# First modulation: the scale summed by columns on TensorE, the shift alone on VectorE

## The chip, the core and the metric

The kernel runs on one core of one Trainium2 chip. The metric is the device time of one execution in microseconds (us); the kernel before has a median of 1437.47 us over 3 runs (1434.62 to 1438.4). One further execution was recorded by the profiler; the rows below come from it.

Engines are written as in the profile: PE is TensorE's matmul, PEld its weight load, DVE is VectorE, ACT is ScalarE, POOL is GpSimd, SP is SyncE, which here only issues transfers.

## The reference, cut to what matters

Two layers, 512 rows of 1024 features, all float32. Each layer begins with a normalization that is modulated by a vector computed from the condition `c`:

```
ada_in = silu(c)
mod  = (ada_in @ w_ada[i] + b_ada[i]).reshape(b, 6, d)
sh_m, sc_m = mod[:, 0], mod[:, 1]
hm = rmsnorm(x, norm_mix[i]) * (1 + sc_m) + sh_m
y  = dilated_mixer(hm, a_w_in[j], ...)
```

The shift `sh_m` and the scale `sc_m` of the first layer are each a product of a vector of 1024 with a matrix of 1024 x 1024 (4 MB). Nothing of the layer can be projected before they are there, so this pair is computed first, in the function `begin`, on its own; the other ten vectors of the two layers are summed in the background later.

## The kernel before, in words

`begin` loads `x` (4 row blocks of 128), then the 8 MB of the scale's and the shift's weights. It works in two halves of 512 features. For each half there are 8 transfers of 512 KB, each with two slices of 128 of the 1024 inputs: first 4 for the scale (n = 0), then 4 for the shift (n = 1). They land in 11 buffers (6 of the tag `mix`, 5 of the tag `ada0`), so that the last five transfers of the second half wait until earlier buffers have been read.

VectorE multiplies each slice by its input (`csil`, one number per partition) and adds it into an accumulator `accs[n]` of 128 partitions (L359). The sum over the 128 partitions is left to TensorE: for each group of 128 features one product with the accumulator's 128 columns as weights and a column of ones as the moving operand (L368), so the result stands as a column, one feature per partition, in PSUM. VectorE then makes the column of scales, (1 + scale) * norm (L371), and copies the column of shifts (L373).

Between, `rows()` squares and scales `x` (ACT, L336, L340), transposes it on PE (L344, 32 products) and copies the result to `xT` (ACT, L345). When the columns of a half are there, ACT makes the high part of `h` for its four groups of 128 features (L376), and VectorE its low part (L377, L378).

After the first half's `h`, PE can begin the first projection with half of its inputs: `project_early` runs 48 products of 128 x 128 by 512 columns (L293, L294, L296: high x high, high x low, low x high) for 4 row blocks into 4 PSUM banks. The rest of that projection needs the second half's `h`. The projection's weights come in a stream (`st`): SP issues the transfers (L114), ACT makes the high part (L150) and VectorE the low part (L151); a buffer is free for the next transfer when L151 has run.

The program is written in this order, and a scheduler places each engine's instructions: earlier lines have priority, but what isn't ready by the scheduler's own reckoning is overtaken. `issue_after(last.ins)` puts L371 and L373 behind the half's last L359 on VectorE. Each engine then runs its list strictly in order.

Of the kernel before, what the change touches and what calls it, by code (L numbers as in the profile page):

```python
# [8 lines left out]
F32 = mybir.dt.float32  # L9
# [4 lines left out]
OP = mybir.AluOpType  # L14
# [3 lines left out]
P = 128  # L18
D = 1024
S = 512  # L20
KT = D // P
# [154 lines left out]
class Trunk:  # L176
# [71 lines left out]
    def cols(self, w, kt0, nk, parts, kind=""):  # L248

        n = sum(m for _, m in parts)  # L250
        src, at = [], 0
        wv = w.rearrange("(kt p) c -> p kt c", p=P)
        for c0, m in parts:
            src.append((wv[:, kt0:kt0 + nk, c0:c0 + m],
                        lambda raw, at=at, m=m: raw[:, :nk * n].rearrange("p (k c) -> p k c", c=n)[:, :, at:at + m]))
            at += m
        return (src, nk * n, kind)
# [41 lines left out]
    def begin(self, sb, first):  # L299

        nc, i, V = self.nc, self.i, self.nc.vector
        c16 = self.k.tile([16, P], F32, name="c16", tag="c16", bufs=1)
        nc.sync.dma_start(out=c16[0:8], in_=i["c"].rearrange("o (k p) -> (o k) p", p=P))
        nc.scalar.dma_start(out=c16[8:16], in_=i["norm_mix"][0].rearrange("(k p) -> k p", p=P))
        self.ident = self.k.tile([P, P], F32, name="ident")
        nc.sync.dma_start(out=self.ident, in_=i["cst"][:, C_I:C_I + P])
        xs = []
        for b in range(NB):
            x = self.k.tile([P, D], F32, name="big", tag="big", bufs=5)
            nc.sync.dma_start(out=x, in_=i["x"][0, b * P:(b + 1) * P, :])  # L310
            xs.append(x)
        self.ones = self.k.tile([P, P], F32, name="ones")
        V.memset(self.ones, 1.0)
        self.one = self.k.tile([P, 1], F32R, name="one")
        nc.scalar.activation(self.one, self.ones[:, 0:1], AF.Copy)
        accs = []
        for n in range(2):
            acc = sb.tile([P, D], F32, name="acc0", tag="acc0", bufs=2)
            nc.gpsimd.memset(acc, 0.0)
            nc.gpsimd.dma_start(out=acc[0:1, :], in_=i["b_ada"][0:1, (1 - n) * D:(2 - n) * D])  # L320
            accs.append(acc)
        t = self.bank("s")
        nc.tensor.transpose(t[:, 0:16], c16, self.ident[0:16, 0:16])
        self.csil = self.k.tile([P, 8], F32, name="csil")
        col = self.k.tile([P, 2, KT], F32, name="col")
        silu = nc.scalar.activation(self.csil, t[:, 0:8], AF.Silu)
        with self.tc.issue_after(silu.ins):
            self.exp_ln()
        V.tensor_copy(col[:, 0], t[:, 8:16])
        xT = sb.tile([P, KT, S], F32, name="xT")  # L330

        def rows():
            ss = self.small(NB, "ss4")
            for b in range(NB):
                sq = sb.tile([P, D], F32, name="sq0", tag="sq0", bufs=1)
                nc.scalar.activation(sq, xs[b], AF.Square, accum_out=ss[:, b:b + 1])  # L336
            V.tensor_scalar(ss, ss, 1.0 / D, EPS, op0=OP.mult, op1=OP.add)
            r = self.rsqrt(ss, NB)
            for b in range(NB):
                nc.scalar.activation(xs[b], xs[b], AF.Copy, scale=r[:, b:b + 1])  # L340
            for k in range(KT):
                t = self.bank("t")
                for b in range(NB):
                    nc.tensor.transpose(t[:, b * P:(b + 1) * P], xs[b][:, k * P:(k + 1) * P], self.ident)  # L344
                nc.scalar.activation(xT[:, k, :], t, AF.Copy)  # L345

        wv = i["w_ada"][0].rearrange("(k p) c -> p k c", p=P)
        for half in range(2):
            cs = slice(half * 512, half * 512 + 512)
            for n in range(2):  # L350
                for kk in range(0, KT, 2):
                    if (8 * half + 4 * n + kk // 2) % 11 < 6:
                        raw = self.k.tile([P, D], F32, name="mix", tag="mix", bufs=6)
                    else:
                        raw = sb.tile([P, D], F32, name="ada", tag="ada0", bufs=5)
                    raw = raw.rearrange("p (k c) -> p k c", c=512)
                    nc.sync.dma_start(out=raw, in_=wv[:, kk:kk + 2, (1 - n) * D + half * 512:(1 - n) * D + half * 512 + 512])
                    for k in range(2):
                        last = V.scalar_tensor_tensor(accs[n][:, cs], raw[:, k], self.csil[:, kk + k:kk + k + 1], accs[n][:, cs], op0=OP.mult, op1=OP.add)  # L359
                if half == 0 and n == 0:  # L360
                    rows()
            if half:
                self.early = self.project_early(first)
            c = slice(4 * half, 4 * half + 4)
            for n in range(2):
                t = self.bank("s")
                for k in range(4 * half, 4 * half + 4):
                    nc.tensor.matmul(t[:, k:k + 1], lhsT=accs[n][:, k * P:(k + 1) * P], rhs=self.ones[:, 0:1], start=True, stop=True)  # L368
                with self.tc.issue_after(last.ins):
                    if n == 0:  # L370
                        V.scalar_tensor_tensor(col[:, 0, c], t[:, c], 1.0, col[:, 0, c], op0=OP.add, op1=OP.mult)  # L371
                    else:
                        V.tensor_copy(col[:, 1, c], t[:, c])  # L373
            for k in range(4 * half, 4 * half + 4):
                hi, lo = self.h(k, slice(None))
                nc.scalar.activation(hi, xT[:, k, :], AF.Identity, scale=col[:, 0, k:k + 1], bias=col[:, 1, k:k + 1])  # L376
                V.tensor_scalar(xT[:, k, :], xT[:, k, :], col[:, 0, k:k + 1], col[:, 1, k:k + 1], op0=OP.mult, op1=OP.add)  # L377
                V.tensor_tensor(lo, xT[:, k, :], hi.bitcast(F32), op=OP.subtract)  # L378
            if half == 0:
                self.st.fill(2)  # L380
# [98 lines left out]
        nc.vector.tensor_scalar(g[:, 0:1], g[:, 0:1], -0.125, None, op0=OP.mult)  # L479
        return g  # L480

    def project_early(self, cols):

        w = [self.st.get(512) for _ in range(2)]
        banks = [self.bank("pj" if b < 3 else "o") for b in range(NB)]
        for b, ps in enumerate(banks):
            for j in range(2):
                self.part(ps, [(*self.h(2 * j + n, cols(b)), *w[j][n]) for n in range(2)], j == 0, False)
                if b == NB - 1:
                    self.st.done()  # L490
        return banks
# [911 lines left out]
```

## Time and profile before

| | |
|---|---|
| median of 3 runs | 1437.47 us (1434.62 to 1438.4) |
| the profiled execution's own time | 1427.06 us |
| its span, first to last instruction | 1425.3 us |
| mean granted TensorE clock | 0.966 |
| PE busy | 1311.6 us (92%) |
| DVE busy | 967.4 us (68%) |
| ACT busy | 652.4 us (46%) |
| POOL busy | 121.0 us (8%) |

The granted clock is a share of full speed: 1.00 stands for 2.4 GHz, 0.50 for 1.2 GHz. A row of a timeline gives the start, the time from there to the end of the last of its instructions, engine, line, output and inputs, shapes and the number of instructions merged; in square brackets stands the idle time before and what ended it. Products are pipelined: the next one starts before the last one's end, so the pitch from start to start is what a stream of them costs.

### The profile page before, as it was taken

What the parts mean: (1) busy time and instruction counts of PE and PEld (TensorE: products, weight loads), DVE (VectorE), ACT (ScalarE), POOL (GpSimd) and SP (SyncE); (2) the same over time, 40 slices, a digit from 0 to 9 for tenths busy, and PEclk for the clock granted to TensorE, in tenths of its full rate; (3) what the DMA queues carried; (4) which work ended last, traced back from release to release, by engine and by line L of the source; (5) the groups of instructions that cost most, each with busy time, mean ns of one, the idle gap of its engine ahead of it and who ended that gap; (6) DMA issues with size and microseconds to landing.
All of it is one profiled execution on the core that took longest, in us unless ns stands there. A gap on an engine that the chain in (4) does not pass through costs nothing. (4 is left out here: it accounts for less than half of the span.)

```text
span 1425.3 us, 20009 instructions
## 1 busy us (share of the span) xinstructions
PE 1311.6 (92%) x7017; PEld 1068.2 (75%) x7017; DVE 967.4 (68%) x1913; ACT 652.4 (46%) x1356; POOL 121.0 (8%) x120
## 2 busy tenths in 40 slices
PE   5899999999998999989979998499999999699995
PEld 4787989888996899878756665268988978566662
DVE  6875776676677676655677775486767854877772
ACT  6433544344435444443355554354554542365560
POOL 0000000000000000000032221000000000223221
PEclk9899999999999999989979999799999999899998
DMA  9465445643554445264789997413321465799981
GB/s 360 138 207 179 153 156 162 202 141 120 169 191 151 161 148 164 82 218 149 254 268 313 294 295 233 148 50 95 112 65 62 134 202 191 258 288 303 302 278 22
DMA packets 187156, 264.14 MB, mean 185 GB/s; under 512 B 23065, under 2 KB 148697, under 8 KB 187047
## 3 DMA queue, kind: packets, MB, share of 16 engines
q1 hardware_dynamic: 160742, 227.86, 48.9%
q0 software_dynamic: 8576, 16.85, 5.0%
q10 hardware_dynamic: 17728, 18.05, 4.3%
q8 instruction: 59, 0.97, 0.3%
q14 instruction: 51, 0.41, 0.1%
HBM read 249.85 MB, written 25.43 MB: 193 GB/s over the span
## 5 line engine op out<-in xcount | busy, mean ns | idle before, releaser
L293 PE MATMUL ps_pj<-hi,h 128*128 128x512 f32 (+1 forms) x1016 | 390.6, 393 | 9.6 <-ACT h L453 5.0
L294 PE MATMUL ps_pj<-lo,h 128*128 128x512 f32 (+1 forms) x1016 | 371.9, 374 | 0.0
L296 PE MATMUL ps_pj<-hi,h 128*128 128x512 f32 (+1 forms) x1016 | 290.0, 374 | 0.0
L293 PEld LDWEIGHTS ps_pj<-hi,h 128*128 128x128 f32 x1016 | 238.6, 235 | 32.7 <-ACT h L453 7.1
L294 PEld LDWEIGHTS ps_pj<-lo,h 128*128 128x128 f32 x1016 | 240.3, 237 | 14.4 <-issue 0.8
L296 PEld LDWEIGHTS ps_pj<-hi,h 128*128 128x128 f32 x1016 | 211.5, 235 | 20.0 <-issue 1.1
L150 ACT ACTIVATE hi<-raw 128x1024 fp32r<-128x1024 f32 x126 | 132.4, 1052 | 130.3 <-PE ps_pj L296 70.7
L151 DVE TENSOR_TENSOR lo<-raw,hi 128x1024 fp32r<-128x1024 f32 x126 | 151.8, 1213 | 48.1 <-ACT hi L150 46.1
L392 DVE SCALAR_TENSOR_TENSOR acc<-ada,csil,acc 128x1024 f32<-128x1024 f32 x80 | 102.6, 1283 | 69.0 <-DMA ada<-in_w_ada 68.8
L293 PE MATMUL ps_pj<-hi,xh 128*112 128x512 f32 x256 | 104.9, 410 | 2.2 <-ACT xh L453 2.2
L294 PE MATMUL ps_pj<-lo,xh 128*112 128x512 f32 x256 | 104.2, 407 | 0.0
L296 PE MATMUL ps_pj<-hi,xl 128*112 128x512 f32 x256 | 80.8, 397 | 0.0
L453 ACT ACTIVATE xh<-ps_t 128x448 fp32r<-128x448 f32 x64 | 31.8, 542 | 81.8 <-PE ps_t L448 75.7
L1235 DVE SCALAR_TENSOR_TENSOR y<-ps_s,r_ws,g_f 112x512 f32<-112x512 f32 x64 | 47.8, 748 | 28.5 <-PE ps_s L1234 28.5
L462 DVE TENSOR_REDUCE qss<-sq 128x8 f32<-128x512 f32 x64 | 43.7, 682 | 31.5 <-ACT sq L460 30.8
L460 ACT ACTIVATE sq<-ps_pj 128x512 f32<-128x512 f32 x63 | 37.1, 589 | 57.7 <-PE ps_pj L296 50.9
L151 DVE TENSOR_TENSOR lo<-h,hi 128x1024 fp32r<-128x1024 f32 x42 | 51.1, 1223 | 15.4 <-ACT hi L150 14.6
L720 PEld LDWEIGHTS ps_o<-vr,pt 128*128 128x128 f32 x480 | 58.6, 193 | 1.4
L720 PE MATMUL ps_o<-vr,pt 128*128 128x64 f32 x480 | 57.8, 272 | 0.0
L293 PEld LDWEIGHTS ps_pj<-hi,xh 128*112 128x112 f32 x256 | 45.5, 178 | 15.4 <-ACT xh L453 3.1
L296 PEld LDWEIGHTS ps_pj<-hi,xl 128*112 128x112 f32 x256 | 44.9, 176 | 15.6 <-DVE xl L454 0.6
L927 ACT ACTIVATE nl<-nl,mn 128x128 f32<-128x128 f32 (+1 forms) x64 | 35.7, 559 | 40.6 <-DVE mn L925 40.1
(280 smaller groups left out, 2176.8 us busy)
## 6 DMA issues: line engine op xcount, KB each, us to landing
ada<-in_w_ada SPq DMA_DIRECT2D x85, 512.0 KB
raw<-in_a_w_in SPq DMA_DIRECT2D x128, 256.0 KB
h<-in_w_gate SPq DMA_DIRECT2D x42, 256.0 KB
h<-in_w_up SPq DMA_DIRECT2D x42, 256.0 KB
mix<-in_w_gate SPq DMA_DIRECT2D x37, 256.0 KB
mix<-in_w_up SPq DMA_DIRECT2D x37, 256.0 KB
raw<-in_w_down SPq DMA_DIRECT2D x18, 512.0 KB
h<-in_w_down SPq DMA_DIRECT2D x18, 512.0 KB
```

The lines of the kernel that those rows point to most:

```text
L150: t.act = nc.scalar.activation(h, r, AF.Copy)
L151: nc.vector.tensor_tensor(l, r, h.bitcast(F32), op=OP.subtract)
L293: nc.tensor.matmul(out, lhsT=hi, rhs=wh, start=first and n == 0, stop=False)
L294: nc.tensor.matmul(out, lhsT=hi, rhs=wl, start=False, stop=False)
L296: nc.tensor.matmul(out, lhsT=lo, rhs=wh, start=False, stop=last and n == len(terms) - 1)
L392: nc.vector.scalar_tensor_tensor(acc, raw, self.csil[:, kt:kt + 1], acc, op0=OP.mult, op1=OP.add)
L453: self.nc.scalar.activation(hv, tv, AF.Copy)
L460: nc.scalar.activation(sq, ps, AF.Square)
L462: nc.vector.tensor_reduce(ss, sq.rearrange("p (h d) -> p h d", d=HD), axis=AX.X, op=OP.add)
L720: nc.tensor.matmul(held["o"][:, at:at + HD], lhsT=pt[:, a * P:(a + 1) * P], rhs=v, start=(m == 0), stop=(m == len(terms) - 1))
L927: nc.scalar.activation(pr[:, sl], pr[:, sl], AF.Exp, scale=-1.0, bias=mn, accum_out=held["d"][:, h * 4 + b:h * 4 + b + 1])
L1235: nc.vector.scalar_tensor_tensor(y[:, cs], yp, m["ws"][0:CAP, e:e + 1], m["g_f"][0:CAP, cs], op0=OP.mult, op1=OP.mult)
```

## The change

The scale's accumulator goes. The scale is summed on TensorE directly: each 128 x 128 block of its weights is the stationary operand and the matching column of `csil` the moving one, 8 slices x 4 groups of features = 32 products of one column for each half, accumulated in PSUM over the slices. The bias is a further small product of 4 rows (`b4`, loaded through ACT's queue). VectorE sums the shift alone, 8 L359 instead of 16 for each half. For the first half the new function `scale` is called ahead of `rows()`; for the second half `project_early` calls it ahead of its third row block.

```diff
-        accs = []
-        for n in range(2):
-            acc = sb.tile([P, D], F32, name="acc0", tag="acc0", bufs=2)
-            nc.gpsimd.memset(acc, 0.0)
-            nc.gpsimd.dma_start(out=acc[0:1, :], in_=i["b_ada"][0:1, (1 - n) * D:(2 - n) * D])
-            accs.append(acc)
+
+        acc = sb.tile([P, D], F32, name="acc0", tag="acc0")
+        nc.gpsimd.memset(acc, 0.0)
+        nc.gpsimd.dma_start(out=acc[0:1, :], in_=i["b_ada"][0:1, 0:D])
+        b4 = sb.tile([4, 2, P], F32, name="b4")
+        nc.scalar.dma_start(out=b4, in_=i["b_ada"][0:1, D:2 * D].rearrange("o (h k p) -> (o k) h p", h=2, p=P))
...
-                    for k in range(2):
-                        last = V.scalar_tensor_tensor(accs[n][:, cs], raw[:, k], self.csil[:, kk + k:kk + k + 1], accs[n][:, cs], op0=OP.mult, op1=OP.add)
-                if half == 0 and n == 0:
-                    rows()
-            if half:
-                self.early = self.project_early(first)
-            c = slice(4 * half, 4 * half + 4)
-            for n in range(2):
+                    raws += [raw[:, k] for k in range(2)]
+
+            def scale():
+
                 t = self.bank("s")
-                for k in range(4 * half, 4 * half + 4):
-                    nc.tensor.matmul(t[:, k:k + 1], lhsT=accs[n][:, k * P:(k + 1) * P], rhs=self.ones[:, 0:1], start=True, stop=True)
-                with self.tc.issue_after(last.ins):
-                    if n == 0:
-                        V.scalar_tensor_tensor(col[:, 0, c], t[:, c], 1.0, col[:, 0, c], op0=OP.add, op1=OP.mult)
-                    else:
-                        V.tensor_copy(col[:, 1, c], t[:, c])
+                nc.tensor.matmul(t[:, c], lhsT=b4[:, half], rhs=self.ident[0:4, 0:4], start=True, stop=False)
+                for kt in range(KT):
+                    for k in range(4):
+                        nc.tensor.matmul(t[:, 4 * half + k:4 * half + k + 1], lhsT=raws[kt][:, k * P:(k + 1) * P], rhs=self.csil[:, kt:kt + 1],
+                                         start=False, stop=(kt == KT - 1 and k == 3))
+                V.scalar_tensor_tensor(col[:, 0, c], t[:, c], 1.0, col[:, 0, c], op0=OP.add, op1=OP.mult)
+
+            for kt in range(KT):
+                last = V.scalar_tensor_tensor(acc[:, cs], raws[KT + kt], self.csil[:, kt:kt + 1], acc[:, cs], op0=OP.mult, op1=OP.add)
+            if half == 0:
+                scale()
+                rows()
+            else:
+                self.early = self.project_early(first, scale)
+            t = self.bank("s")
+            for k in range(4 * half, 4 * half + 4):
+                nc.tensor.matmul(t[:, k:k + 1], lhsT=acc[:, k * P:(k + 1) * P], rhs=self.ones[:, 0:1], start=True, stop=True)
+            with self.tc.issue_after(last.ins):
+                V.tensor_copy(col[:, 1, c], t[:, c])
...
-    def project_early(self, cols):
+    def project_early(self, cols, between):
...
         for b, ps in enumerate(banks):
+            if b == 2:
+                between()
```

## Rows read from the trace of the kernel before

**Rows 1.** The page's first part: busy time of each engine over the span.

```profile
PE 1311.6 (92%) x7017; PEld 1068.2 (75%) x7017; DVE 967.4 (68%) x1913; ACT 652.4 (46%) x1356; POOL 121.0 (8%) x120
```

**Rows 2.** Stretches: length, busy time of each engine (instructions), granted clock, transfers.

```profile
10.75:17.25 6.50, 2.40 (x8) 1.19 (x9) 6.29 (x13) 4.68 (x6) 0.00 (x0) 1.00 1.05 408
17.25:25.50 8.25, 8.25 (x42) 7.42 (x40) 5.90 (x9) 5.02 (x9) 0.00 (x0) 1.00 1.07 379
...
28.15:31.60 3.45, 3.45 (x10) 2.82 (x9) 3.45 (x7) 1.72 (x3) 0.00 (x0) 0.51 1.05 408
...
40.10:49.50 9.40, 2.52 (x17) 2.37 (x16) 8.84 (x13) 2.86 (x4) 0.00 (x0) 0.78 0.38 116
49.50:55.50 6.00, 5.99 (x13) 4.38 (x14) 5.97 (x10) 3.13 (x4) 0.00 (x0) 0.50 1.07 324
...
910.00:920.00 10.00, 3.00 (x11) 2.74 (x12) 6.17 (x14) 7.88 (x19) 0.00 (x0) 0.50 0.51 203
```

**Rows 3.** Timeline of PE, first half of the modulation.

```profile
17.40 1.71 PE L368 MATMUL ps_s<-ones,acc 128*128 128x1 f32 x8
18.97 5.55 PE L344 MATMUL ps_t<-ident,big 128*128 128x128 f32 x24
24.32 1.19 PE L368 MATMUL ps_s<-ones,acc 128*128 128x1 f32 x8
```

**Rows 4.** Timeline of PE, second half of the modulation.

```profile
38.77 0.40 PE L294 MATMUL ps_o<-lo,h 128*128 128x512 f32 x1
39.01 0.40 PE L293 MATMUL ps_o<-hi,h 128*128 128x512 f32 x1
...
41.52 1.05 PE L368 MATMUL ps_s<-ones,acc 128*128 128x1 f32 x8 [1.40 <-DVE acc L359]
...
49.51 0.81 PE L293 MATMUL ps_pj<-hi,h 128*128 128x512 f32 x1 [3.20 <-ACT h L376]
...
54.33 0.63 PE L293 MATMUL ps_pj<-hi,h 128*128 128x512 f32 x1
54.75 0.63 PE L294 MATMUL ps_pj<-lo,h 128*128 128x512 f32 x1
```

**Rows 5.** Timeline of PE at two other places: transposes of the same shape.

```profile
64.11 0.27 PE L655 MATMUL ps_t<-J,qn 128*128 128x128 f32 x1
64.22 0.27 PE L656 MATMUL ps_t<-ident,qn 128*128 128x128 f32 x1
...
917.00 1.97 PE L448 MATMUL ps_t<-ident,hm 128*128 128x128 f32 x8 [16.71 <-DVE hm L430]
```

**Rows 6.** Timeline of DVE: sums of the modulation, and the last column.

```profile
12.47 7.71 DVE L359 SCALAR_TENSOR_TENSOR acc<-mix,csil,acc 128x512 f32<-128x512 f32 x10
20.21 3.12 DVE L359 SCALAR_TENSOR_TENSOR acc<-ada,csil,acc 128x512 f32<-128x512 f32 x4
...
38.73 4.19 DVE L359 SCALAR_TENSOR_TENSOR acc<-mix,csil,acc 128x512 f32<-128x512 f32 x6
...
48.11 0.15 DVE L373 COPY col<-ps_s 128x4 f32<-128x4 f32 x1
```

**Rows 7.** Timeline of ACT: the first part of h, of either half.

```profile
26.00 1.51 ACT L376 ACTIVATE h<-xT,col 128x512 fp32r<-128x512 f32 x2
...
48.66 1.50 ACT L376 ACTIVATE h<-xT,col 128x512 fp32r<-128x512 f32 x2
```

**Rows 8.** Timeline of SP's queue: the second half's last five transfers.

```profile
19.79 3.50 SPq L357 DMA_DIRECT2D mix<-in_w_ada  x5
```

**Rows 9.** Line 368: engine, operation, number; shortest, median, longest ns; first and last start.

```profile
L368 PE MATMUL ps_s<-ones,acc x32: 208/250/353, 17.4 to 46.0; 128*128 128x1 f32 x32
```

**Rows 10.** Waits: who for whom, us in total, times, longest.

```profile
SPq L114 <- DVE lo L151: 11.2, 3, 9.5
...
PE ps_s L404 <- ACT ada L397: 5.2, 3, 2.3
...
PE ps_t L655 <- DVE rs_t L215: 1.6, 1, 1.6
```

More of the change, by code (lines that the diff above doesn't have):

```diff
@@ L348, in begin @@
         for half in range(2):
-            cs = slice(half * 512, half * 512 + 512)
+            cs, c = slice(half * 512, half * 512 + 512), slice(4 * half, 4 * half + 4)
+            raws = []
             for n in range(2):
```

## Prediction, made before the changed kernel was run

> **What bounds the kernel now.** I read the busy times first: PE works 92% of the span [rows 1], so time is mostly won or lost where PE waits, and work that is added to PE is time wherever PE doesn't. The change touches the first 60 us, so I cut these into stretches by the timeline of PE and asked for each engine's busy time and the granted clock in each [rows 2]. From 10.75 to 17.25 PE works 2.40 of 6.50 us: the scale's first weights are there, VectorE sums them (6.29 us of 6.50), PE idles 4.1 us. From 17.25 to 25.50 PE is full (8.25 of 8.25) with the transposes and the two groups of L368 [rows 3]; 0.5 us after the last of these ACT begins the first h, at 26.00 [rows 7]. Then PE runs the 48 products of the early projection up to 40.1. From 40.1 to 49.5 it works 2.52 of 9.40 us while VectorE is full (8.84): here VectorE is the bound, with the second half's L359 and the L151 between them [rows 2, 6]. The column of shifts comes at 48.11, h at 48.66, PE's next product at 49.51 [rows 4, 6, 7].
>
> The clock matters as much. Stretch 49.5 to 55.5 is granted 0.50, the 1.2 GHz level, after the idle 40.1 to 49.5; products of 512 columns go at a pitch of 0.42 us there (54.33, 54.75), against 0.24 at 1.00, 2.4 GHz (38.77, 39.01) [rows 2, 4]. In the first 25 us the column reads 1.00 as well, but I don't believe it there: 24 transposes take 5.55 us, 0.23 each [rows 3], eight take 1.97 us, 0.25 each, in a stretch granted 0.50 [rows 2, 5], and two at 64 us, granted 1.00, start 0.11 apart [rows 5]. So PE runs at the low level until the last transposes, although it was busy without a gap from 17.25.
>
> **What the change removes.** 16 of 32 L359. Fourteen of them took 10.83 us at 12.47 to 23.33, 0.77 each; six later ones 4.19, 0.70 each [rows 6]: 11 to 12 us off VectorE. Only the second half's 8, some 5.6 us, lie on the path. In the first half VectorE ends at 23.33 while PE goes on to 25.51 [rows 3, 6], so these 8 are worth nothing by themselves. One POOL fill and one transfer of 4 KB go too, on an engine that works 8% [rows 1]: nothing.
>
> **What it adds.** Line 368 makes 16 products in the code and 32 in the trace [rows 9]: a float32 product is two passes, each with its own load of 128 columns of weights. So the 64 new products are 128 passes, and the two of `b4` 4 more: 66 for each half, less 8 of L368 that go. A pass is the same operation as L368's (128 x 128 weights, one column), so its price is in the trace, at either level: eight at 17.40 take 1.71 us and the last of them alone 0.35, so (1.71 - 0.35) / 7 = 0.19 us; eight at 41.52 take 1.05 and 0.21, so 0.12 us [rows 3, 4, 9]. The two levels are the bounds of all that follows.
>
> The Trainium skill, "TensorEngine Tiling (Array Packing)", section Instruction Overhead, puts a matmul at some 60 cycles whatever it has below 60 columns; that would be 25 ns a pass at 2.4 GHz, 1.5 us for 58, hidden in PE's idle 4.1. Its page "TensorE: Matmul & The Clock Gate", section LDWEIGHTS (loading the stationary operand), puts a load of 128 columns at 128/1.2 = 107 ns, 6.2 us for 58. The row at 41.52 (0.12) sides with the second, so a product of one column is paid by its weights.
>
> **First half, to the first h.** 58 passes more: 11.0 us at 0.19, 7.0 at 0.12. They can begin with the first weights, at 10.75, and PE has 4.1 us of idle time from there to 17.25 [rows 2], so 6.9 or 2.9 us remain; at the upper level the 24 transposes would shrink too (0.11 for 0.22, 2.6 us), which leaves 0.3. Which one? No row shows a long run of one-column passes. PE starts at the low level and stayed there in a full stretch of transposes and passes until about 24.5 (the eight passes at 24.32 take 1.19 us, not 1.71) [rows 3], so I take the low price, less 0.9 us for a rise of the clock during the last transposes and L368: **+6.0** (0.3 to 6.9). If the scheduler puts transposes first, the sum is the same, since h needs both.
>
> **Second half, 40.1 to 48.66.** These 8.6 us become 66 + 8 passes and the 0.5 us from the last L368 to h. At 0.12 that is 9.4 us (+0.8), at 0.19 14.6 (+6.0). The passes stand between row blocks 1 and 2; PE comes to them at the upper level from dense products. The clock fell to 0.51 at 28.15, after eight passes, 1.35 us of idle time and a few products [rows 2, 3]; I expect it to fall in the course of 66 passes and take the middle, +3.4. If it falls, the 24 products of row blocks 2 and 3 begin low: 0 to 24 x (0.42 - 0.24) = 4.3, half of it 2.2. Sum **+5.6** (0.8 to 10.3). VectorE, 5.6 us lighter, is done with its L359 before 40 and covered by PE.
>
> **After h.** The 6.0 us at 0.50 (49.5 to 55.5) cost 13 products some 2.9 us over 13 x 0.24 [rows 2, 4]. With PE working up to the last L368, only a gap like that of 25.5 to 26.85 is left, and after that one the clock was down for 3.45 us [rows 2], 1.7 us lost. So **-1.2** (0 to -2.9).
>
> **Further on.** SP's queue waits 11.2 us for L151 in the first 70 us, and transfers stand nearly still (0.38 of the engines' time) from 40.1 to 49.5 [rows 2, 10]. VectorE, lighter, frees the buffers sooner, and PE comes later, so weights are more likely there when PE arrives. Between 56 and 300 us PE waits 1.6 us behind a late norm and 5.2 us for background sums [rows 10]; the first is the nearest, **-1.6** (0 to -6.8).
>
> **At nothing.** `b4` is one issue on ACT's queue before ACT has its rows of x, half a microsecond at most, covered by the transposes that now wait for PE anyway. The second half's last five transfers reuse buffers that PE, not VectorE, now frees (SP issues them at 19.79 to 23.29 [rows 8]); at the low price PE is done with them around 25, some 2 us late, with the stream's weights behind them on SP. That lies under PE's own delay.
>
> **Sum.** 6.0 + 5.6 - 1.2 - 1.6 = +8.8 us; all lows give -8.6, all highs +17.2. On the profiled execution's 1427.06 us that is 1435.9. The median of the runs is 10.4 us above the profiled one; I carry the difference over: 1437.5 + 8.8 = **1446.3 us**.
>
> **The rivals.** A difference of 0.3%, 4.3 us, is about what a measurement of this kernel can tell from none.
>
> *The passes keep the clock up.* From 10.75 PE is now dense, so the clock might rise by about 18, as it did some 7 us after PE became full at 17.25 [rows 2, 3], and then stay. The first half then costs +0.5, the second +0.8, and the stretch after h gives 2.0: -0.7, 1437. Against it: the full stretch that stayed low, and the fall at 28.15. Chance 0.20, no change. The Trainium skill's page "TensorE: Matmul & The Clock Gate", section on what you observe, says that activity releases the throttle; by that rule this rival is the outcome. The traces so far don't show whether one-column passes are enough activity.
>
> *The delay is caught up further on.* All as forecast, but the 6.8 us of waits at 78.90 and in the background sums vanish, since weights and sums run ahead of a late PE: 8.8 - 5.2 = +3.6, 1441. For it: VectorE's relief. Against it: PE is full in most of that time, and these waits follow transfers that are issued as buffers come free, hence follow PE. Chance 0.11, no change.
>
> *Faster: transfers restart earlier.* If the passes cost 0.12 throughout, the early part ends even, and VectorE, which frees the stream's buffers some 5.6 us sooner, gets the transfers going in the hole from 40.1 to 49.5 [rows 2]; then the waits above go and nothing is lost before: -0.7 - 5.2 = -5.9, 1431.6. It decides only if the price is the upper level's and the holes do matter. Chance 0.09.
>
> The forecast has 0.60. Slower by over 0.3%: 0.60; within: 0.31; faster: 0.09. For 8 in 10 I leave out the fast rival and the upper end of the bounds: 1435.5 to 1454.5. The likeliest case's own range is 1442 to 1454.
>
> **What the profile would show.** Two groups of 66 one-column passes; right, if each takes over 9 us, the first h begins at 31 to 33 us and the second at 58 to 62, VectorE idles between 38 and 48, and the granted clock falls during the second group or right behind it. Wrong, if transposes in the first 25 us start 0.11 apart (clock up early), if the second group takes 8 us at 1.00, or if PE's waits from 56 to 300 us shrink by more than 4 us. The scheduler could also place the passes where I don't expect them, into waits before the first h, and then the second half would cost less.

## Result, and the profile after

The changed kernel has a median of 1447.96 us over 4 runs (1446.43 to 1450.36); the kernel before, on the same chip, 1436.59 over 4 (1434.62 to 1438.4). The ratio is 1.0081, 95% interval 1.0059 to 1.0103: slower by 11.4 us, where 8.8 were forecast. The profiled execution took 1450.36 us, its span is 1448.6; against before's 1427.06 that is 23.3 us, twice the difference of the medians; the run of before_again and the part on the prediction come back to that.

The page's first part of after, to hold against [rows 1]:

```profile
PE 1340.7 (93%) x7133; PEld 1093.1 (75%) x7133; DVE 957.9 (66%) x1897; ACT 652.3 (45%) x1356; POOL 119.8 (8%) x118
```

116 more passes on PE, 16 fewer instructions on DVE, and 29 us more busy time on PE. The timeline of PE of after, for the first half and then the second (L367 are the new passes, L380 the shift's sums over the partitions, L634 the product that was L623, L666 the transpose that was L655):

```profile
10.89 6.96 PE L367 MATMUL ps_s<-csil,mix 128*128 128x1 f32 x32 [6.98 <-DMA mix<-in_w_ada]
17.71 1.09 PE L344 MATMUL ps_t<-ident,big 128*128 128x128 f32 x4
18.59 3.41 PE L367 MATMUL ps_s<-csil,mix 128*128 128x1 f32 x16
21.87 0.67 PE L344 MATMUL ps_t<-ident,big 128*128 128x128 f32 x2
22.33 3.41 PE L367 MATMUL ps_s<-csil,mix 128*128 128x1 f32 x16
25.60 0.67 PE L344 MATMUL ps_t<-ident,big 128*128 128x128 f32 x2
26.74 5.35 PE L344 MATMUL ps_t<-ident,big 128*128 128x128 f32 x24 [0.47 <-ACT xT L345]
32.27 1.02 PE L380 MATMUL ps_s<-ones,acc 128*128 128x1 f32 x8 [0.18 <-issue]
...
39.52 4.59 PE L367 MATMUL ps_s<-csil,ada 128*128 128x1 f32 x32
43.97 0.77 PE L293 MATMUL ps_pj<-hi,h 128*128 128x512 f32 x1
...
48.80 1.84 PE L367 MATMUL ps_s<-csil,ada 128*128 128x1 f32 x16
50.51 2.02 PE L367 MATMUL ps_s<-csil,mix 128*128 128x1 f32 x16
52.39 0.78 PE L294 MATMUL ps_pj<-lo,h 128*128 128x512 f32 x1
...
59.36 0.95 PE L380 MATMUL ps_s<-ones,acc 128*128 128x1 f32 x8
...
77.01 0.80 PE L634 MATMUL ps_s<-oh,rb 33*16 33x384 f32 x2 [1.92 <-DMA rb<-in_rel_bias]
...
80.72 0.47 PE L666 MATMUL ps_t<-J,qn 128*128 128x128 f32 x1 [2.05 <-DVE qn L477]
```

In the first half the 64 passes take 6.82 + 3.28 + 3.27 = 13.4 us from start to next start, 0.21 each; the 24 transposes cost what they cost before [rows 3]. In the second half the last 32 take 1.71 + 1.88 us; the first 16 of these are 0.107 each. The same kind of pass stands in one trace at two prices, a factor of two apart.

Stretches of after (length, busy time of each engine, granted clock, transfers), for [rows 2]:

```profile
17.25:25.50 8.25, 8.25 (x41) 8.25 (x42) 0.00 (x0) 0.00 (x0) 0.00 (x0) 1.00 1.07 380
39.50:44.00 4.50, 4.50 (x34) 4.48 (x32) 0.89 (x2) 0.00 (x0) 0.00 (x0) 0.77 0.41 117
44.00:48.80 4.80, 4.80 (x12) 3.78 (x13) 0.00 (x0) 0.00 (x0) 0.00 (x0) 0.50 0.00 0
48.80:52.40 3.60, 3.60 (x34) 3.60 (x32) 0.00 (x0) 0.00 (x0) 0.00 (x0) 0.97 0.00 0
52.40:55.50 3.10, 3.10 (x8) 2.48 (x9) 2.83 (x5) 0.00 (x0) 0.00 (x0) 0.50 0.00 0
55.50:59.40 3.90, 3.90 (x19) 3.82 (x17) 3.26 (x5) 0.00 (x0) 0.00 (x0) 0.98 0.00 0
...
61.50:66.00 4.50, 4.50 (x12) 3.78 (x13) 4.24 (x7) 4.50 (x6) 0.00 (x0) 0.62 0.56 175
```

PE is full in all of them, so the hole of 40.1 to 49.5 is gone. But the clock falls in the course of the first 32 passes and again with the last 16, and both times the products of 512 columns behind them run at 1.2 GHz. VectorE, ACT and the transfers do nothing from 44.0 to 48.8. The reading of 1.00 ahead of 25 us is again not to be believed: passes of 0.21 are the low level's (in late_scale below sixteen take 3.55 us, 0.22 each, in a stretch granted 0.50). PEld, the load of the weights, is busy in all of 17.25 to 25.50: the passes follow each other as fast as their loads.

The timelines of VectorE and then of ACT show who waits (L369 makes the scale's column, L372 sums the shift, L382 copies the shift's column, L385 makes h):

```profile
25.78 0.16 DVE L369 SCALAR_TENSOR_TENSOR col<-ps_s,col 128x4 f32<-128x4 f32 x1 [13.97 <-PE ps_s L367]
25.91 3.11 DVE L372 SCALAR_TENSOR_TENSOR acc<-mix,csil,acc 128x512 f32<-128x512 f32 x4
...
52.57 0.16 DVE L369 SCALAR_TENSOR_TENSOR col<-ps_s,col 128x4 f32<-128x4 f32 x1 [12.14 <-PE ps_s L367]
52.65 6.25 DVE L372 SCALAR_TENSOR_TENSOR acc<-mix,csil,acc 128x512 f32<-128x512 f32 x8
60.34 0.16 DVE L382 COPY col<-ps_s 128x4 f32<-128x4 f32 x1 [1.44 <-PE ps_s L380]
```

```profile
33.59 1.52 ACT L385 ACTIVATE h<-xT,col 128x512 fp32r<-128x512 f32 x2
...
60.60 0.81 ACT L385 ACTIVATE h<-xT,col 128x512 fp32r<-128x512 f32 x1 [22.18 <-DVE col L382]
61.32 1.04 ACT L150 ACTIVATE hi<-raw 128x1024 fp32r<-128x1024 f32 x1
...
74.34 0.60 ACTq L627 DMA_DIRECT2D rb<-in_rel_bias  x1
```

The scale's column stands ahead of the shift's sums on VectorE, and VectorE idles 13.97 and 12.14 us, although the sums have their data for much of that time (in col_last below they run from 16.4 us on). ACT stands 22.18 us for the second half's h with the weights' L150 queued behind it, and behind these the issue of `rb`'s load, which L634 waits for. So no buffer of the stream comes free; the waits of SP's queue up to 85 us show it, against 11.9 us before in the same stretch (11.2 of them up to 70 us [rows 10]):

```profile
SPq L114 <- DVE lo L151: 33.4, 7, 22.0
```

The first h begins at 33.59 instead of 26.00, the second at 60.60 instead of 48.66 [rows 7]: +7.6 and +11.9. As a mark behind them I take the first product of the background sums, L404 before and L413 after. The two rows are of different kernels, before first (shortest, median and longest ns; first and last start):

```profile
L404 PE MATMUL ps_s<-ada,one x3: 390/391/400, 101.3 to 139.8; 128*1 128x512 f32 x3
```

```profile
L413 PE MATMUL ps_s<-ada,one x2: 398/402/407, 116.0 to 116.2; 128*1 128x512 f32 x2
```

101.3 has become 116.0: +14.7, more than the medians differ by. In this pair of traces the whole of that difference is there by 116 us.

### The profile page after: what moved, and what is told of

Its sections match the earlier page's. It is cut to its first block, busy times and chain, and to the rows that moved or that the text cites. A ratio compares the mean times of both kernels' runs of the same rounds, so it can differ in the third digit from the quotient of the medians.

```text
span 1448.6 us, 20219 instructions
## 1 busy us (share of the span) xinstructions
PE 1340.7 (93%) x7133; PEld 1093.1 (75%) x7133; DVE 957.9 (66%) x1897; ACT 652.3 (45%) x1356; POOL 119.8 (8%) x118
## 5 line engine op out<-in xcount | busy, mean ns | idle before, releaser
L150 ACT ACTIVATE hi<-raw 128x1024 fp32r<-128x1024 f32 x126 | 132.3, 1051 | 109.4 <-PE ps_pj L296 69.8
L151 DVE TENSOR_TENSOR lo<-raw,hi 128x1024 fp32r<-128x1024 f32 x126 | 151.6, 1213 | 42.2 <-ACT hi L150 41.4
L151 DVE TENSOR_TENSOR lo<-h,hi 128x1024 fp32r<-128x1024 f32 x42 | 51.1, 1223 | 15.5 <-ACT hi L150 13.5
L294 PEld LDWEIGHTS ps_pj<-lo,xh 128*112 128x112 f32 x256 | 45.7, 178 | 11.9 <-issue 0.5
```

The source lines that it names most:

```text
L150: t.act = nc.scalar.activation(h, r, AF.Copy)
L151: nc.vector.tensor_tensor(l, r, h.bitcast(F32), op=OP.subtract)
L294: nc.tensor.matmul(out, lhsT=hi, rhs=wl, start=False, stop=False)
```

## The experiments

Three causes were to be told apart: the passes' time on PE (with the clock that goes with them), VectorE's wait with the column ahead of the sums, and the order of the lists on ACT and VectorE, which holds the weights' stream. The changes are shown against the changed kernel unless another is named; ratios and medians are against the kernel before on the same chip (23 runs per chip, medians 1432.31, 1433.32 and 1433.11 us). The changed kernel was timed only in the comparison of the result above, so its 1.0081 was not measured beside the ratios below.

**The kernel before once more**, one execution.

> The kernel before once more, for a second profile. The two profiled spans differ by 23.3 us (1425.3 and 1448.6) where the medians differ by 11.4. If the first profile of before was a fast one, this one spans some 1433 to 1437 us, with the first 62 us unchanged (first h at 26.0, second at 48.7) and some 8 to 10 us more further on, after 270 us. If instead the change costs 23 us in any profile, it spans 1425 to 1428.

1427.19 us, span 1425.4, clock 0.964; first h at 26.45, second at 49.03. The profiled execution of before comes out the same again, which is the expectation's branch in which the change costs 23 us in any profile. The timed runs speak against that branch: the 23 of before in this comparison lie between 1422.82 and 1439.68, both profiled executions near the low end, and the profiled executions of the versions below lie on either side of their medians. The end of a single trace can't stand for a median. Times inside the first 60 us agree within half a microsecond in these two traces; one trace below (mixed) runs 1.5 us late as a whole.

**Each half alone.** The scale goes to PE in half 0 only, or in half 1 only; in the other half VectorE sums both vectors as before.

```diff
+HALF_ON_PE = 0        # first_half; 1 in second_half
...
+                    if half != HALF_ON_PE:
+                        for k in range(2):
+                            last = V.scalar_tensor_tensor(accs[n][:, cs], raw[:, k], ...)
...
+            if half == HALF_ON_PE:
...
+                if half == 0:
+                    scale()
+                    rows()
+                else:
+                    self.early = self.project_early(first, scale)
```

> Only the first half's scale is summed on TensorE; the second half as before, both sums on VectorE. Theory passes (TensorE's one-column passes at the low clock level set the end): the first h stays at 33.6 us as in the changed kernel, PE full from 10.9 to 33; the second h then at 56 to 57 (48.7 + 7.6); 7 to 8 us slower than before, 3 to 4 faster than the changed kernel. Theory stall (VectorE's list, where the scale's column stands ahead of the shift's sums, sets it): most of the delay comes from the second half, where transfers stand still; this kernel is slower than before by 4 us at most.

> Only the second half's scale is summed on TensorE; the first half as before. Theory passes: first h at 26.0 as before, second h at 52 to 54 (48.7 + 4.3), the granted clock falling to 0.50 during or right behind the passes; 4 to 5 us slower than before. Theory stall: VectorE stands some 12 us for the column, transfers stand from about 38 us on, and the loss behind the second h (3.3 us in the changed kernel) comes here as well: 7 us slower or more.

First half alone: 1.0045 (1.0024 to 1.0065), 1439.86 us; h at 34.03 and 56.47, the mark at 108.9 (+7.6). Second half alone: 1.0061 (1.0034 to 1.0088), 1439.93 us; h at 26.18 and 54.85, the mark at 110.2 (+8.9). Either half costs, and in the traces the two add up (16.5 against 14.7). What differs is the stretch behind h. The first half's delay of 7.8 us at the second h is still 7.6 at the mark: nothing is caught up and nothing lost. The second half's 6.2 at h grows to 8.9. There ACT stands for the column, as in after:

```profile
54.85 0.81 ACT L401 ACTIVATE h<-xT,col 128x512 fp32r<-128x512 f32 x1 [19.01 <-DVE col L398]
```

In the trace with the first half alone the same h comes without such a wait. So the loss behind h belongs to the second half's edit. second_half's 7.6 us in the medians is the number that its expectation gave for the stall, not the 4 to 5 for the passes; the next run tests what the stall on VectorE is worth.

**The scale's column behind the shift's sums**, which takes VectorE's 13.97 and 12.14 us of waiting away.

```diff
-                V.scalar_tensor_tensor(col[:, 0, c], t[:, c], 1.0, col[:, 0, c], op0=OP.add, op1=OP.mult)
+                with self.tc.issue_after(last.ins):
+                    V.scalar_tensor_tensor(col[:, 0, c], t[:, c], 1.0, col[:, 0, c], op0=OP.add, op1=OP.mult)
```

> The changed kernel, but on VectorE the scale's column is put behind the shift's sums of its half, so that they don't wait for TensorE. Theory passes: the shift's sums end at about 22 us in the first half instead of 32.2, yet the first h stays at 33.3 to 33.6 and the second at 60 to 60.6, since TensorE ends its transposes at 32.1 and its fourth row block at 59.5 anyway; at most 3 us are won behind the second h; so 0 to 3 us faster than the changed kernel. Theory stall: the second h comes 3 us or more earlier, and this kernel is within 4 us of before.

1.012 (1.0085 to 1.0154), 1449.99 us: no faster. The first half on VectorE and PE:

```profile
19.56 3.12 DVE L373 SCALAR_TENSOR_TENSOR acc<-ada,csil,acc 128x512 f32<-128x512 f32 x4
25.95 0.16 DVE L370 SCALAR_TENSOR_TENSOR col<-ps_s,col 128x4 f32<-128x4 f32 x1 [3.27 <-PE ps_s L367]
```

```profile
26.92 5.12 PE L344 MATMUL ps_t<-ident,big 128*128 128x128 f32 x24 [0.47 <-ACT xT L345]
31.87 0.95 PE L381 MATMUL ps_s<-ones,acc 128*128 128x1 f32 x8
```

The shift's sums end at 22.7 instead of 32.2, and the first h comes at 33.51 instead of 33.59: PE reaches the transposes no sooner. In the second half the sums end at 46.55, then VectorE waits 3.72 and 8.27 us for PE, and h comes at 58.95, 1.65 earlier. At the mark 0.8 us of that is left (115.2). VectorE's long wait in after is for the most part a consequence; what it waits for, PE with its passes, is the cause.

**Half of the passes.** Every other slice of the scale is left out, so that this kernel sums the scale over half of the inputs only; all else stays.

```diff
-                for kt in range(KT):
+                for kt in range(0, KT, 2):
...
-                                         start=False, stop=(kt == KT - 1 and k == 3))
+                                         start=False, stop=(kt == KT - 2 and k == 3))
```

> The changed kernel with every other slice of the scale left out on TensorE: 32 instead of 64 passes in each half (its scale is therefore a sum over half of the inputs). All else, VectorE's lists among it, stays. Theory passes: 32 fewer passes at 0.21 us win 6.8 us ahead of the first h (33.6 to about 27) and 32 at 0.11 to 0.14 some 4 more ahead of the second (60.6 to 48 to 50): 10 to 12 us faster than the changed kernel, even with before. Theory stall (the lists' order): transfers still stand and ACT still waits for the column ahead of the weights, so less than 6 us are won.

1.0009 (0.9986 to 1.0033), 1433.47 us: the whole loss is gone, where the versions with all 64 passes on the same chip (warm, lists, late_scale) are 9.8 to 19.5 us slower than before. PE in the first half:

```profile
10.99 3.54 PE L367 MATMUL ps_s<-csil,mix 128*128 128x1 f32 x16 [7.11 <-DMA mix<-in_w_ada]
14.39 1.09 PE L344 MATMUL ps_t<-ident,big 128*128 128x128 f32 x4
15.28 1.71 PE L367 MATMUL ps_s<-csil,mix 128*128 128x1 f32 x8
```

32 passes fewer bring the first h from 33.59 to 26.94: 6.65 us, 0.21 a pass, which is the price in the rows, with nothing hidden. The second h comes at 47.37 and the mark at 103.0, 1.6 us behind before: the loss behind h stays. So the cost does not begin at the first pass: the 32 that stay in the first half take 6.8 us, of which PE's idle 4.1 [rows 2] and the 1.7 of the eight L368 that went [rows 3] cover all but 1.0, and the first h is 0.9 later than before.

**PE busy beforehand.** 18 products of ones with ones, 128 columns each, right after the first transpose, to raise the clock before the first weights land.

```diff
-        nc.tensor.transpose(t[:, 0:16], c16, self.ident[0:16, 0:16])
+        tr = nc.tensor.transpose(t[:, 0:16], c16, self.ident[0:16, 0:16])
+        busy = self.bank("t")
+        with self.tc.issue_after(tr.ins):
+            for _ in range(18):
+                nc.tensor.matmul(busy[:, 0:P], lhsT=self.ones, rhs=self.ones, start=True, stop=True)
```

> The changed kernel with 18 more products of a tile of ones (36 passes of 128 columns) on TensorE from 3.5 us on, into a bank that nobody reads, so that the clock may be up when the scale's weights land. If one-column passes keep the clock up, all 64 of the first half go at 0.11 (7 us) and the first h comes at 25 to 27 us. If they let it fall, the first 20 to 40 passes are fast, the rest and the transposes slow: first h at 29 to 32. If the added products don't raise the clock at all, it stays at 33.6.

1.0071 (1.0040 to 1.0102), 1443.09 us. PE:

```profile
3.32 6.22 PE L327 MATMUL ps_t<-ones 128*128 128x128 f32 x36
...
11.39 4.37 PE L371 MATMUL ps_s<-csil,mix 128*128 128x1 f32 x32 [1.55 <-ACT rs_y L214]
15.62 1.09 PE L348 MATMUL ps_t<-ident,big 128*128 128x128 f32 x4
16.51 3.41 PE L371 MATMUL ps_s<-csil,mix 128*128 128x1 f32 x16
```

The first 32 passes take 0.13 each instead of 0.21, the next 16 are back at 0.21. The clock was up when they began, behind 1.55 us of idle time, and fell while PE did nothing but passes (granted 1.00 from 13 to 14 us, 0.62 from 14 to 15, 0.50 from there). The first h gains 2.1 us (31.51) and no more. In the median the gain is inside the intervals.

**The second half's passes placed elsewhere**: behind all four row blocks instead of between the second and the third (late_scale); eight at a time behind each half of a row block (spread; `scale` then yields after each slice); the latter with the second half alone on PE (second_spread, which is spread's edit on second_half).

```diff
         for b, ps in enumerate(banks):
-            if b == 2:
-                between()
             for j in range(2):
                 self.part(ps, ...)
...
+                next(between, None)      # spread
+        between()                        # late_scale
```

> The changed kernel with the second half's passes behind all four row blocks of the early projection instead of ahead of the third. Theory passes, with the clock as the second part of the price: no product of 512 columns follows the passes before the second h, so the fall of the clock costs fewer of them: the fourth row block ends at 47 to 49, the passes take 8 to 11 us, the second h comes at 58 to 60 (60.6 in the changed kernel), and some of the win goes again behind it, where the clock is now low; 0 to 2 us faster in all. If the fall of the clock in row blocks 2 and 3 cost nothing, the second h stays at 60.6.

> The changed kernel with the second half's 64 passes in eight groups of 8, each behind 6 products of the early projection, instead of in one block. If it is a long run of one-column passes that lets the clock fall, it stays up here: the passes cost 0.11 us each, the last two row blocks run at a pitch of 0.24, and the second h comes at 56 to 58 instead of 60.6. If the clock falls for another reason, or spreading costs as much as it saves, the second h stays at 60 to 61. The first h stays at 33.6. In all 2 to 4 us faster than the changed kernel, still slower than before.

> Only the second half's scale on TensorE, in the same eight groups; the first half as before. First h at 26.2, second at 49 to 52 (54.9 with the passes in one block). By the theory of passes and clock, TensorE has 7 to 8 us more work at the upper level where before it waited 7 us for VectorE, so the second h is within 2 us of before; what is lost behind it (2.8 us with the passes in one block, from the lists' order) may remain. 0 to 5 us slower than before in all.

All three expectations were missed on the slow side. late_scale: 1.0145 (1.0108 to 1.0182), 1452.83 us, second h at 61.65; its last 16 passes take 3.55 us, so the clock fell there too, and two of the shift's sums, which stood behind the scale's column on VectorE, held L380 for 1.80 us more. spread: 1.0124 (1.0085 to 1.0163), 1451.9 us, second h at 64.84, 4.2 us later than in after. One of its stretches, and its passes at either level:

```profile
46.00:50.00 4.00, 4.00 (x15) 3.55 (x14) 0.00 (x0) 0.00 (x0) 0.00 (x0) 0.50 0.00 0
```

```profile
43.86 1.70 PE L367 MATMUL ps_s<-csil,ada 128*128 128x1 f32 x8
...
53.48 0.95 PE L367 MATMUL ps_s<-csil,ada 128*128 128x1 f32 x8
```

PE is full from 38 to 54 with products among which passes are strewn, and the clock stays at 0.50 to about 52, where it rises behind a stretch of products alone. Once it is up, four more groups of eight leave it up (0.95 us each). second_spread: 1.0062 (1.0034 to 1.0090), 1441.72 us, h at 56.08 where second_half had 54.85. Here six of the eight groups come at the upper level, and passes and products end at 51.4. But three of the shift's sums stand behind the scale's column on VectorE, and PE waits for them (in spread 1.80 us for two):

```profile
53.95 1.84 PE L396 MATMUL ps_s<-ones,acc 128*128 128x1 f32 x8 [2.58 <-DVE acc L383]
```

So spreading alone does not hide the passes; what it would give with the sums ahead of the column was not tried, and these runs don't show it.

**The lists.** The weights' L150 and L151 that were overtaken are put ahead of the second half's h on ACT and of its shift column on VectorE; the scale's column goes behind the sums, as above.

```diff
-            with self.tc.issue_after(last.ins):
+            with self.tc.issue_after(self.low.ins if half else last.ins):
                 V.tensor_copy(col[:, 1, c], t[:, c])
...
-                nc.scalar.activation(hi, xT[:, k, :], AF.Identity, ...)
+                with self.tc.issue_after(self.act.ins) if half else nullcontext():
+                    nc.scalar.activation(hi, xT[:, k, :], AF.Identity, ...)
```

> The changed kernel with the scale's column behind the shift's sums, and in the second half VectorE's copy of the shift's column and ACT's h put behind the weights' high and low parts that are already issued, as they ran in the kernel before. The first h stays at 33.5 and the second at 59 to 60.6, both set by TensorE. What the changed kernel lost behind the second h (anchor L623 of before, L634 of after: +15.2 us, against +11.9 for the second h) should go if ACT's and VectorE's lists caused it: anchor at +10 to +12, total 3 to 4 us faster than the changed kernel. If that loss was the clock's or the transfers' alone, the anchor stays at +14 to +15.

1.0104 (1.0069 to 1.0139), 1445.89 us. ACT's wait for the column shrinks, and PE no longer waits for `rb`:

```profile
63.16 0.81 ACT L387 ACTIVATE h<-xT,col 128x512 fp32r<-128x512 f32 x1 [1.36 <-DVE col L383]
```

At the expectation's anchor, the product with `rb`, the delay against before is 12.7 us (74.51) instead of 15.2, between its two branches. But h comes at 63.16, 2.6 us later than in after, and the mark at 116.4, no earlier than after's 116.0. The lists say where the wait is paid, ahead of h or behind it; they are not a loss on top that can be taken away by this order. (VectorE still stood 6.04 us for the scale's column, with L151 behind it. An order in which that wait goes too was not tried.)

**A part of the scale on PE.** The kernel before, with 4 of the scale's 8 slices of the second half taken by PE, behind the early projection, into the hole there.

```diff
-                    for k in range(2):
+                    for k in range(0 if half and n == 0 and kk >= 4 else 2):
                         last = V.scalar_tensor_tensor(accs[n][:, cs], ...)
...
+                    more = range(4, KT) if half and n == 0 else ()
+                    for kt in more:
+                        nc.tensor.matmul(t[:, k:k + 1], lhsT=raws[kt][:, (k - 4) * P:(k - 3) * P], rhs=self.csil[:, kt:kt + 1], start=kt == 4, stop=False)
```

> The kernel before, but in the second half TensorE sums four of the scale's eight slices, as 32 one-column passes behind the early projection, where it waited for VectorE; VectorE makes 12 sums there instead of 16. If TensorE's idle time is what makes a pass free and VectorE is the bound there, the second h comes 2 to 3 us earlier than before (46 to 47 instead of 48.7), the total 0 to 3 us faster than before, hardly more than can be measured. If passes are paid even there, or the lists change for the worse, it is not faster.

0.9983 (0.9958 to 1.0008), 1431.42 us: no difference that these runs can tell. PE in the hole:

```profile
41.80 0.58 PE L372 MATMUL ps_s<-csil,mix 128*128 128x1 f32 x4
...
43.61 0.99 PE L372 MATMUL ps_s<-csil,ada 128*128 128x1 f32 x4
44.47 0.99 PE L372 MATMUL ps_s<-csil,mix 128*128 128x1 f32 x4
```

The passes begin at 0.11 (the next instruction starts at 42.24) and are at 0.21 two microseconds later; VectorE, 2.8 us lighter, then waits 5.02 us for them, and h comes at 50.02. That is 1.4 us behind before, but in this execution ACT's squares wait for a late load of `x`, and the first h, which the edit doesn't touch, comes 1.5 us late too (27.48): ahead of the second h the trace shows neither a gain nor a cost of the edit. Behind h this trace loses 4.2 us more, and the mark stands at 106.9, 5.5 behind before; yet the median is not slower. So a delay at the mark of one trace need not be found again in the median; where it went is open. No version tried is faster than the kernel before.

## Why the prediction was right, by its own steps

The forecast was 1446.3 us and the likeliest case came: slower, since a pass is paid by its load of weights. That the total was only 2.6 us off is in part luck: the first half came out 1.6 us above its term and the stretch behind h 3.9 above, the second half 1.3 below, and what is left of the medians' difference behind the mark (11.4 - 14.7 = -3.3) lies 1.7 below. That last figure sets a trace against medians and is no measurement.

**The price of a pass.** The bounds 0.12 and 0.19 were right in kind. They came out of one row each by taking the last pass's full time off, and the long groups correct them: 0.107 (1.71 us for 16) and 0.21 (6.82 us for 32). The Trainium skill, "TensorE: Matmul & The Clock Gate", section LDWEIGHTS (loading the stationary operand), gives P/1.2 ns for P columns, an estimate of 107 ns for 128; the upper level's 0.107 agrees, the lower takes twice that. The estimate of 25 ns from the Trainium skill, "TensorEngine Tiling (Array Packing)", section Instruction Overhead, is not the price of a pass in any row of L367; that section says nothing of a load of weights, and here each pass brings one.

**First half, forecast +6.0, measured +7.6.** Right mechanism, mis-sized term. 13.4 us of passes, less the 1.7 of L368's eight that went [rows 3], less the 4.1 of idle time they fill [rows 2], make 7.6. I had 11.0 for the first two, 0.7 too little, and took 0.9 off for a rise of the clock that gained nothing: the 24 transposes take 5.35 us, against 5.55 before, and 0.47 of idle time stands ahead of them. half_passes confirms the price by taking passes away, and col_last excludes VectorE's wait.

**Second half, forecast +5.6, measured 11.9 - 7.6 = +4.3.** The passes themselves take 4.45 + 1.71 + 1.88 = 8.0 us and from the last L380's start at 59.36 to h it is 1.2: 9.3 in place of 8.6, so +0.7, where I had +3.4 (its low bound, +0.8, was the right one). What the clock does to the products around them is larger than the 2.2 allowed: in the timeline 11 products start between 43.97 and 48.80 and 7 between 52.39 and 55.53, 18 in 8.0 us against 18 x 0.24 = 4.3 [rows 4]: 3.7 us lost, near the upper bound of 4.3. The clock fell twice, not once.

**After h, forecast -1.2, measured 14.66 - 11.94 = +2.7 up to the mark.** This step failed, though the saving in it came: between 61.47 and 66.07, where the clock is low behind the gap of 1.16 us, 12 products of 512 columns take 4.6 us, 1.7 more than 12 x 0.24, as forecast, against 2.9 lost before. What I had not costed are the lists. ACT's h stands ahead of the weights' L150, and VectorE's column ahead of the sums, so the weights' transfers stand still from 44 to 59.4, and `rb`'s load, which ACT issues behind its L150, starts at 74.34, so that PE waits 1.92 us for it, then 2.05 for `qn`. Behind these waits the clock is low a third time, 0.50 from 80.7 to 86.3; two microseconds of that stretch (PE alone, granted clock, transfers):

```profile
82.00:84.00 2.00, 2.00 (x8) 0.50 0.20 76
```

From the first product behind h to the mark PE idles 4.2 us, against 2.7 before, and 203 instructions in either trace keep it busy for 50.3 us, against 49.1: together the +2.7. From the second h to the mark it is 52.7 us in before, 52.5 in first_half and 53.2 in lists; in the nine traces in which ACT's h waits for the column with L150 behind it, it is 54.2 to 56.9. I had named a different placing of the passes as a danger, not a different order on the two other engines. That the scheduler put them there because it reckons the passes cheap fits, but was only argued.

**Further on, forecast -1.6.** PE's waits between 56 and 300 us did not shrink: they sum to 10.3 us before and to 10.4 in after without the one for h. Of after:

```profile
PE ps_s L413 <- ACT ada L406: 3.8, 2, 2.0
PE ps_t L666 <- DVE qn L477: 2.9, 4, 2.0
```

The background sums cost 1.4 us less than before [rows 10], and `qn` and `rb` take that back. In the profiled pair 8.6 us more are lost behind the mark, in the medians none are. Executions of before lie up to 17.6 us apart on one chip, its profiled one at their low end and after's at the high end of its four, so this remainder is not a cost of the change that these runs show; what moves it from execution to execution stays open.

**The rivals.** That the passes keep the clock up is refuted from both sides: in after PE is full of passes and transposes from 10.89 to 26.3 and the passes stay at 0.21, and in warm the clock is raised first and falls among them. By the rule in the Trainium skill, "TensorE: Matmul & The Clock Gate", section What's actually happening (not What you observe, as I had it), that activity releases the throttle, this rival would have come; these two traces do not agree with it. That the delay is caught up is refuted for the first half's delay by first_half, whose 7.8 us at h are 7.6 at the mark and 7.55 in the medians; for what is lost behind h, mixed leaves it open. The fast rival needed the upper level throughout and transfers that restart earlier; they restarted later.

**The signs.** The second h (60.60), VectorE's idle time and the clock's fall in the second group came as named, and the first h at 33.59, 0.6 us outside of 31 to 33. Two signs did not: the passes came in three pieces in the first half and two in the second, and the second group's take 8.0 us in all, not over 9, the length that was named as a sign of being wrong, though not at 1.00 throughout (granted 0.77, then 0.97). It was the products around them, at the low level, that made up the second half's delay.

## What to carry to other kernels

A float32 product of one column is two passes, and each costs the load of its 128 columns of weights, 0.107 us at 2.4 GHz and 0.21 at 1.2, so a matrix that is used for one vector is no bargain on TensorE unless the engine would idle anyway: count the passes, multiply by the slow price, and take off only the idle time that the rows show at that place. Count also what happens to the products behind them: in the second half here the low clock cost these 3.7 us, where the passes themselves, in place of VectorE's sums, cost 0.7. And when a step moves from one engine to another, look what the new wait stands in front of on the engine that only copies the result. A sum that comes out near the total says little for its terms: hold each of them against the trace.

## What the runs showed of the hardware that was not expected

- In streams of one-column passes without a gap the granted clock fell, though PE counts as fully busy: at about 42 us in after, in warm after at most 32 passes (with 1.55 us of idle time ahead of them), in mixed at about 43.5. In second_spread it fell at about 39.2, among products of 512 columns, a microsecond behind two groups of eight passes. A PE that the rows show as full was granted either level (in after 0.50 from 44.0 to 48.8, 0.98 from 55.5 to 59.4).
- From the low level, products of 512 columns mixed with groups of eight passes ran some 14 us without the clock rising (spread, 38 to 52 us). At the upper level the same mixture went on at 1.00 from 52.5 to 62 in spread, and fell to the low level in second_spread.
- A pass with its load of 128 columns of weights and one column of product takes twice as long at the low level (0.21 against 0.107 us), so the clock matters for passes that are all load as much as for wide products.
